# A list scheduler that counts TensorE's tile changes, operand changes and weight loads

## The chip, the cores and the metric

The kernel runs on one core of a Trainium2 chip. The metric is device time in microseconds (us) of one execution; the median of three runs is given, and one further execution was profiled. TensorE (PE) multiplies matrices; its weight loads are listed apart (PEld). VectorE (DVE), ScalarE (ACT) and GpSimd (POOL) do elementwise work; SyncE (SP) issues nearly all transfers.

## The reference, cut to what matters

One layer of a hybrid backbone over 640 tokens: 512 noisy grid tokens that see a cached context, and 128 prompt tokens. An adaLN-modulated input is projected by one wide matrix; four mixers run side by side (latent attention MLA, bidirectional mLSTM, windowed attention SWA, bidirectional RWKV-7); each passes an output matrix and a sigmoid gate; their sum passes `w_out`; a squared-ReLU MLP follows.

```python
h = rmsnorm(x, P['norm1'][l]) * (1.0 + scale1) + shift1
u = h @ P['w_in'][l]                       # 1024 x 8752, split into the mixers' inputs and 4 x 1024 gates
...
def step(Sm, inp):                         # RWKV-7, one token, one head (64 x 64 state)
    sk = jnp.einsum('bhvk,bhk->bhv', Sm, kh_t)
    Sn = Sm * w_t[:, :, None, :] - sk[..., None] * (a_t * kh_t)[:, :, None, :] + v_t[..., None] * k_t[:, :, None, :]
    return Sn, jnp.einsum('bhvk,bhk->bhv', Sn, r_t)
...
merged = (gates[:, :, 0] * (y_a @ P['mla_w_o'][l]) + gates[:, :, 1] * (y_b @ P['mlstm_w_o'][l])
          + gates[:, :, 2] * (y_c @ P['swa_w_o'][l]) + gates[:, :, 3] * (y_d @ P['rwkv_w_o'][l]))
x = x + gate1 * (merged @ P['w_out'][l])
f = jnp.square(jax.nn.relu(h2 @ P['mlp_w1'][l])) @ P['mlp_w2'][l]
```

All is float32, with tight tolerances, so the large products are made in three passes of the fast float32r type (high times high, high times low, low times high), and the small ones in plain float32.

## The kernel before, in words

**Dense products.** Weights come in pieces of up to 528 columns: a transfer into one of 3 buffers `wr`, ScalarE makes the high part `wh`, GpSimd (the first 139 pieces) or VectorE the low part `wl` (6 buffers each). `dense_b` (L614) makes channel-major results, in rows named `pb`: 128 weight columns stationary, two halves of 320 tokens moving, 48 matmuls for 128 channels. `dense_t` (L634) makes token-major ones, rows `pt`: 128 tokens stationary, up to 264 weight columns moving. `pa` and `pwo` are the MLP's second product and the output projection, with 512 columns. All of them are float32r and use the whole 128 x 128 array.

**Small products** are plain float32 and mostly use part of the array. Each is two records in the profile. In the RWKV chain (`step`, L1101; rows `pst`) one chunk of 64 tokens of a head pair and a direction takes a product of `S` and `KR` (128 x 128), then `VU` with `Am` (64 x 64), a copy by ScalarE (`W1`, L1115), `W1` with `Am` (64 x 64), a copy by VectorE (`VU`, L1118), `VU` with `Am` and with `KBT` (128 rows by 64 columns), and an update of `S` by VectorE (L1124), from which the next chunk starts. Four head pairs run one after the other; in each, two directions run interleaved over 8 chunks that depend on each other, beside 2 of the prompt. `psf` transposes the state at a pair's end. Preparation (`pat`, `pkb`) and a triangular inverse (VectorE, `ltmp` and `xl`, then `ptp` and `px` in 32 x 32 tiles) go ahead of each pair. Later stages: SWA (`psc`, `pspt`, `pso`) beside mLSTM (`pms`, `pmo`), then MLA's projections (`pq`, `pkv`) and attention (`pas`, `pat` again, here with `avM` and `aPT`), then the merge (`pb` on `yh`, `yl`). The dense projections of the gates and of later mixers (`fill_all`, `late`) have two accumulators of their own and may run at any time in between, in the order of their weights' buffers.

**What sets the order.** The program is first recorded, and `order` (L168) then puts it in order by a list schedule: it plays all engines forward with durations from `cost` (L127) and latencies between engines (L36, L37), and lets each engine take, among the instructions that are ready, the one with the longest path to the end (`bl`, with additions for work that empties PSUM and for stores). On TensorE the played time knows that a matmul must wait for those in flight only where their parts of the array overlap (`busy`), and that the next one may start 0.02 us later (`free`, L462). It also plays the clock: `seen` adds up the columns of work in each window of 3.41 us, and a window after one with fewer than 3060 runs at half speed (`warm`, L408). Where the present window is about to miss that, it takes the ready matmul with the most columns per time (L428) instead. The order found is then fixed on every engine; semaphores alone decide the times.

## Time and profile before

| | |
|---|---|
| three runs, us | 1810.11, 1816.44, 1823.94 (median 1816.44) |
| profiled execution | 1829.33 us; span from its first to its last instruction 1827.4 us |
| mean granted TensorE clock | 0.960 |
| busy, share of the span | PE 95%, PEld 85%, DVE 53%, ACT 39%, POOL 26% |
| instructions of them | 11923, 11923, 2250, 1711, 488 |
| matmuls with the whole array, 320 columns (`pb` on `HH`, `HL`) | 3 x 1328, 321 to 325 ns each, start to end |

A matmul's length in the profile reaches over the start of the next one, so what a matmul costs is read from the distance between two starts. A form such as `128*64 128x64` is rows times columns of the array that it uses, then partitions by elements that it reads. "Idle" is time in which an engine ran nothing; the granted clock is the share of full speed that TensorE had.

### The profile page before, as it was taken

The numbers are of one execution on the slowest core, as the hardware profiler recorded it, in microseconds if no ns is written. First come the engines' busy times: TensorE is split into PE (matmuls) and PEld (weight loads), VectorE is DVE, ScalarE is ACT, GpSimd is POOL, SyncE is SP. The second block draws the span as 40 slices with busy tenths as digits, with TensorE's granted clock in tenths as the row PEclk, the third lists the DMA queues.
The fourth block names the chain that finished last, engine by engine and source line by source line (L and its number), as shares of the span: only waits on it lengthen the run. The fifth ranks groups of instructions, "written<-read, shape, count | busy, mean of one in ns | idle before, by whom it ended". The sixth has DMA issues, their size and how long they took to land.

```text
span 1827.4 us, 32001 instructions
## 1 busy us (share of the span) xinstructions
PE 1742.4 (95%) x11923; PEld 1551.1 (85%) x11923; DVE 968.7 (53%) x2250; ACT 716.9 (39%) x1711; POOL 471.9 (26%) x488
## 2 busy tenths in 40 slices
PE   6999899999999987999989999899999999999998
PEld 3998788888888876878887999799889899898997
DVE  4236937586363348665548654367744334343342
ACT  5543242333223224675635643354434223132231
POOL 3455543354233223331222211005100010202012
PEclk9999999898679998999999999999999999999999
DMA  8554352344224354533363211576512222222222
GB/s 291 153 180 122 103 132 74 90 118 108 64 59 122 114 170 149 168 89 65 86 159 105 74 41 56 167 253 221 173 45 81 68 77 70 81 76 75 76 74 94
DMA packets 243211, 206.66 MB, mean 113 GB/s; under 512 B 46086, under 2 KB 194360, under 8 KB 243056
## 3 DMA queue, kind: packets, MB, share of 16 engines
q1 hardware_dynamic: 242416, 204.07, 38.2%
q8 instruction: 94, 1.54, 0.4%
q0 software_dynamic: 640, 0.56, 0.1%
q14 instruction: 61, 0.50, 0.1%
HBM read 163.08 MB, written 41.49 MB: 112 GB/s over the span
## 4 chain that ended last, share of the span: by engine, by line
PE 57%; DVE 5%; DMA 5%; ACT 1%; issue 1%; SPq 0%; POOL 0%; POOLq 0%; DVEq 0%; ACTq 0%
PE pb L542 29%; PE pa L542 12%; PE pwo L542 2%; DMA out_new_mlstm_n<-co 2%; PE pst L542 2%; PE pas L542 2%; PE pat L542 2%; PE pat L565 1%; PE pso L542 1%; PE pmo L542 1%; PE psc L542 1%; PE pada L542 1%; DMA wr<-in_w_in 1%; PE pms L542 1%; PE pspt L565 0%
## 5 line engine op out<-in xcount | busy, mean ns | idle before, releaser
L542 PE MATMUL pb<-HH,wh 128*128 128x320 f32 x1328 | 364.1, 325 | 21.8 <-ACT spb L833 10.8
L542 PE MATMUL pb<-HL,wh 128*128 128x320 f32 x1328 | 359.5, 323 | 0.8 <-DVE HL L753 0.8
L542 PE MATMUL pb<-HH,wl 128*128 128x320 f32 x1328 | 356.0, 321 | 0.0
L589 ACT CAST wh<-wr 128x512 fp32r<-128x512 f32 (+2 forms) x298 | 183.5, 618 | 379.9 <-PE pa L542 144.2
L592 POOL TENSOR_TENSOR wl<-wr,wh 128x512 fp32r<-128x512 f32 (+2 forms) x139 | 187.4, 1352 | 415.0 <-ACT wh L589 307.8
L542 PEld LDWEIGHTS pb<-HH,wh 128*128 128x128 f32 x1328 | 237.5, 192 | 33.6 <-ACT spb L833 12.9
L542 PEld LDWEIGHTS pb<-HL,wh 128*128 128x128 f32 x1328 | 236.8, 192 | 7.3 <-issue 4.0
L542 PEld LDWEIGHTS pb<-HH,wl 128*128 128x128 f32 x1328 | 236.4, 192 | 6.3 <-issue 3.5
L592 DVE TENSOR_TENSOR wl<-wr,wh 128x512 fp32r<-128x512 f32 x159 | 117.4, 744 | 200.1 <-ACT wh L589 116.5
L1846 POOL TENSOR_TENSOR x<-x,yt 128x512 f32<-128x512 f32 x40 | 53.6, 1341 | 480.7 <-DVE yt L1845 473.7
L542 PE MATMUL pt<-wh,HH 128*128 128x256 f32 (+2 forms) x360 | 101.7, 318 | 7.8 <-DVE mift L860 5.4
L542 PE MATMUL pa<-wh,fh 128*128 128x512 f32 x320 | 108.1, 393 | 0.0
L542 PE MATMUL pa<-wh,fl 128*128 128x512 f32 x320 | 106.7, 393 | 0.0
L542 PE MATMUL pa<-wl,fh 128*128 128x512 f32 x320 | 104.9, 393 | 0.0
L542 PE MATMUL pt<-wh,HL 128*128 128x256 f32 (+2 forms) x360 | 97.9, 312 | 0.0
L542 PE MATMUL pt<-wl,HH 128*128 128x256 f32 (+2 forms) x360 | 96.8, 310 | 0.0
L1109 POOL TENSOR_SCALAR S<-S,DL 128x128 f32<-128x128 f32 x80 | 56.8, 714 | 126.9 <-DVE S L1124 100.3
L542 PEld LDWEIGHTS pt<-wh,HH 128*128 128x128 f32 x360 | 68.1, 206 | 13.6 <-DVE mift L860 3.0
L835 DVE COPY spb<-pb 128x320 f32<-128x320 f32 x46 | 22.4, 487 | 105.9 <-PE pb L542 105.7
L542 PE MATMUL pst<-VU,Am 128*64 128x64 f32 (+1 forms) x640 | 74.2, 242 | 0.9 <-DVE VU L1118 0.5
L542 PE MATMUL pb<-yh,wh 128*128 128x320 f32 x256 | 64.8, 318 | 10.0 <-ACT yh L1752 6.5
L542 PEld LDWEIGHTS pa<-wh,fh 128*128 128x128 f32 x320 | 60.1, 188 | 13.4
(535 smaller groups left out, 3587.0 us busy)
## 6 DMA issues: line engine op xcount, KB each, us to landing
wr<-in_mlp_w SPq DMA_DIRECT2D x128, 256.0 KB
wr<-in_w_in SPq DMA_DIRECT2D x122, 256.0 KB
wa<-in_ada_w SPq DMA_DIRECT2D x64, 256.0 KB
gtd<-spb SPq DMA_DIRECT2D x32, 320.0 KB
sg<-gtd SPq DMA_DIRECT2D x32, 320.0 KB
ara<-in_ada_w SPq DMA_DIRECT2D x16, 512.0 KB
sgd<-sg SPq DMA_DIRECT2D x16, 320.0 KB
la<-sgd SPq DMA_DIRECT2D x16, 320.0 KB
```

What stands on the lines that cost most here:

```text
L542: PE.matmul(out, lhsT, rhs, start=start, stop=stop)
L565: PE.transpose(out, in_, ident[: in_.shape[0], : in_.shape[0]])
L589: A.copy(hi[:, :n], raw[:, :n])
L592: e.tensor_tensor(lo[:, :n], raw[:, :n], hi[:, :n].bitcast(F32), op=ALU.subtract)
L835: V.tensor_copy(t[:, hs(h)], p)
L1109: G.tensor_scalar(sn, so_, DL[:, c : c + 1], None, op0=ALU.mult)
L1846: G.tensor_tensor(x2[tt][:, cs], x2[tt][:, cs], t, op=ALU.add)
```

## The change

It is all in `cost` and `order`. The price of a float32r matmul goes from n/2400 us (at least 0.107) + 0.003 to n/2300 + 0.008 (at least 0.111), that of a plain one from n/600 + 0.002 to the larger of n and (n + m)/2, over 600, + 0.005, m being the columns of the array. Each matmul gets a form: its tile, rows and columns rounded up to 32, 64 or 128, and whether it is plain float32. A matmul of another tile than the one before waits in the played time for all in flight and 0.14 us more; a plain one after another kind in the same tile 0.08 us more. The next matmul may start after the weight load (columns/1200 us, twice that for plain float32), no longer after 0.02. In the choice by columns per time, that charge counts as time. Where the window's work is not in danger, a ready matmul of another tile must have a path to the end that is over 40 us longer (`STAY`) to be taken.

```diff
--- before.py
+++ after.py
@@ -35,6 +35,7 @@
 
 LAT = {"PE": 0.3, "DVE": 0.195, "Activation": 0.195, "Pool": 0.195}
 TO_PE = 0.127
+STAY = 40.0
 DMA_START, DMA_END, DMA_RATE, DMA_GAP = 1.5, 0.95, 360e3, 0.641
 
 
@@ -144,9 +145,9 @@
         if "is_transpose=True" in str(i):
             return 0.109
         if "float32r" in str(i.ins[0].dtype):
-            return max(n / 2400, 0.107) + 0.003
-        return max(n / 600, 0.05) + 0.002
-        
+            return max(n / 2300 + 0.008, 0.111)
+        return max(n, (n + m) / 2) / 600 + 0.005
+
     n = max([free(q) for q in ins + outs] or [1])
     if eng == "Activation":
         if op == "InstLoadActFuncSet":
@@ -406,6 +407,14 @@
         passes = 2 if "is_transpose=True" in str(raw[a]) else 1 if "float32r" in str(i.dtype) else 4
         cols[a] = passes * n * (spot[a][1] - spot[a][0]) / 128
     warm = lambda t: seen.get(int(t / TICK) - 1, 0) >= 3060
+    fit = lambda n: 32 if n <= 32 else 64 if n <= 64 else 128
+    form, load = {}, {}
+    for a, (r0, r1, c0, c1) in spot.items():
+        slow = "is_transpose=True" not in str(raw[a]) and "float32r" not in str(raw[a].ins[0].dtype)
+        form[a] = (fit(r1 - r0), fit(c1 - c0)), slow
+        load[a] = (c1 - c0) / 1200 * (2 if slow else 1)
+    now = ((128, 128), False)
+    turn = lambda a: 0.14 if form[a][0] != now[0] else 0.08 if form[a][1] and not now[1] else 0.0
     while left:
         best = None
         for e in ENG:
@@ -425,7 +434,9 @@
         if e == "PE" and (0.937 or 0) and len(avail[e]) > 1:
             gap = 3060 - seen.get(int(t / TICK), 0)
             if (not warm(t) and 0) or gap > ((int(t / TICK) + 1) * TICK - t) * 2400 * 0.937 > 0:
-                j = max(range(len(avail[e])), key=lambda i: (cols[avail[e][i][1]] / dur[avail[e][i][1]], -avail[e][i][0]))
+                j = max(range(len(avail[e])), key=lambda i: (cols[avail[e][i][1]] / (dur[avail[e][i][1]] + turn(avail[e][i][1])), -avail[e][i][0]))
+            else:
+                j = min(range(len(avail[e])), key=lambda i: avail[e][i][0] + (STAY if form[avail[e][i][1]][0] != now[0] else 0.0))
         if j:
             _, a = avail[e].pop(j)
             heapq.heapify(avail[e])
@@ -449,7 +460,9 @@
         else:
             if e == "PE":
                 r0, r1, c0, c1 = spot[a]
-                t = max([t] + [x[4] for x in busy if x[0] < r1 and r0 < x[1] and x[2] < c1 and c0 < x[3]])
+                other = form[a][0] != now[0]
+                t = max([t] + [x[4] for x in busy if other or x[0] < r1 and r0 < x[1] and x[2] < c1 and c0 < x[3]]) + turn(a)
+                now = form[a]
                 start[a] = t
                 w = warm(t)
                 fin = t + dur[a] * (1 if w else 2)
@@ -459,7 +472,7 @@
                     seen[k] = seen.get(k, 0) + cols[a] * (y - x) / (fin - t)
                     k, x = k + 1, y
                 busy = [x for x in busy if x[4] > t + 0.02] + [(r0, r1, c0, c1, fin)]
-                free[e] = t + 0.02
+                free[e] = t + max(0.02, min(fin - t, load[a] * (1 if w else 2)))
             else:
                 fin = free[e] = t + dur[a]
         out[e].append(a)
@@ -477,6 +490,7 @@
             need2[b] -= 1
             if need2[b] == 0:
                 release(b)
+    order.span = max(free.values())
     info = mybir.DependencyInfo(mybir.DependencyClass.NoSync, mybir.DependencyReason.DATA)
     for e in ENG:
         for a, b in zip(out[e], out[e][1:]):
```

TensorE's order, in the chain of head pair 0. `pst_969` and `pst_974` are the same chunk step (the fifth) of the two directions; `pb` and `pt` are dense projections. A row with "x2" is two products. Before:

```order
L542 MATMUL pb_272_1963<-HL_65,wh_277_1995 128x320
L542 MATMUL pst_969_5901<-W1_970_5905,Am_756_4989 64x64 x2
L542 MATMUL pb_272_1963<-HH_64,wl_276_1994 128x320
L542 MATMUL pst_974_5923<-S_962_5875,KR_770_5053 128x128
L542 MATMUL pb_272_1963<-HH_64,wh_277_1995 128x320
L542 MATMUL pst_974_5923<-VU_973_5920,Am_772_5062 64x64 x2
L542 MATMUL pb_280_2028<-HH_64,wh_283_2031 128x320
L542 MATMUL pb_272_1963<-HL_65,wh_277_1995 128x320
L542 MATMUL pb_280_2028<-HL_65,wh_283_2031 128x320
L542 MATMUL pst_969_5901<-VU_968_5898,Am_756_4989 64x64 x2
L542 MATMUL pst_969_5901<-VU_968_5898,KBT_757_4990 64x64 x2
```

Now, the same small products:

```order
L556 MATMUL pt_244_1717<-wl_230_1665,HH_64 128x264
L556 MATMUL pst_974_5923<-S_962_5875,KR_770_5053 128x128
L556 MATMUL pst_969_5901<-W1_970_5905,Am_756_4989 64x64 x2
L556 MATMUL pst_974_5923<-VU_973_5920,Am_772_5062 64x64 x2
L556 MATMUL pt_244_1717<-wh_234_1672,HH_64 128x264
L556 MATMUL pt_242_1689<-wh_234_1672,HH_64 128x264
L556 MATMUL pt_244_1717<-wh_234_1672,HL_65 128x264
L556 MATMUL pt_242_1689<-wh_234_1672,HL_65 128x264
L556 MATMUL pst_969_5901<-VU_968_5898,Am_756_4989 64x64 x2
L556 MATMUL pst_969_5901<-VU_968_5898,KBT_757_4990 64x64 x2
```

Before, single dense products stand between the small ones, and the tile changes five times in these rows. Now the three small products of the two directions stand side by side, the dense ones come four at a time, and the tile changes three times; the dense work beside this step is another piece of the projections (`pt`) than before (`pb`).

TensorE's order in MLA's attention, for one pair of heads: `aPT` holds the transposed probabilities, `avM` the values, `pat_2572` is where their products add up. Before:

```order
L542 MATMUL pat_2572_13271<-avM_10832,aPT_2569_13258 128x64
L542 MATMUL pb_2232_11643<-HH_64,wh_2235_11646 128x320
L542 MATMUL pat_2572_13271<-avM_10832,aPT_2569_13258 128x64
L542 MATMUL pb_2233_11644<-HL_65,wh_2235_11646 128x320
L542 MATMUL pat_2572_13271<-avM_10832,aPT_2569_13258 128x64
L542 MATMUL pb_2232_11643<-HL_65,wh_2235_11646 128x320
L542 MATMUL pat_2572_13271<-avM_10832,aPT_2569_13258 128x64
L542 MATMUL pb_2233_11644<-HH_64,wl_2234_11645 128x320
L542 MATMUL pat_2572_13271<-avM_10832,aPT_2569_13258 128x64 x2
```

Now:

```order
L556 MATMUL pas_2600_13414<-akT_10831,qTm_2398_12374 128x128
L556 MATMUL pb_2188_11314<-HL_65,wh_2193_11346 128x320
L556 MATMUL pat_2572_13271<-avM_10832,aPT_2569_13258 128x64 x3
L579 MATMUL pat_2581_13320<-k0_68,aP_2578_13311 128x128 x4
L556 MATMUL pat_2572_13271<-avM_10832,aPT_2569_13258 128x64 x6
L579 MATMUL pat_2582_13326<-k0_68,aP_2576_13300 128x128
L579 MATMUL pat_2582_13326<-k0_68,aP_2578_13311 128x128
L556 MATMUL pat_2572_13271<-avM_10832,aPT_2569_13258 128x64
L556 MATMUL pb_2187_11313<-HL_65,wh_2193_11346 128x320
```

Before, each product with `avM` (plain float32) has a dense `pb` (float32r) behind it. Now they come three and six in a row, behind transposes, and the dense work stands together.

Over the whole order, the dense products that stand ahead of some points change, too: ahead of the end of chain 2 (the last `psf` of head pair 2) there were 745 `pb` and 1080 `pt`, and now there are 663 and 480.

## The prediction

> **What bounds the kernel now.** I read the page first, then the stretches, then the chain of waits and the waits by engine, then single matmuls in order of time.

> The page's head, and its rows of 40 slices for TensorE and its clock:

> ```profile
> span 1827.4 us, 32001 instructions
> PE 1742.4 (95%) x11923; PEld 1551.1 (85%) x11923; DVE 968.7 (53%) x2250; ACT 716.9 (39%) x1711; POOL 471.9 (26%) x488
> PEclk9999999898679998999999999999999999999999
> ```

> TensorE is busy for 95% of the span, so its instruction stream sets the time. The clock's row has one deep hole, in slices 11 and 12 (457 to 548 us). The busy times by stretch of the span:

> ```profile
> core 0: us, PE busy (x) PEld busy (x) DVE busy (x) ACT busy (x) POOL busy (x), PEclk, DMA share, GB/s
> 115.00:557.00 442.00, 424.96 (x3514) 371.13 (x3513) 287.31 (x618) 142.51 (x316) 190.84 (x183) 0.90 0.37 99
> 360.00:428.00 68.00, 67.70 (x650) 57.25 (x649) 55.47 (x138) 22.77 (x63) 37.17 (x36) 1.00 0.35 100
> 428.00:557.00 129.00, 125.59 (x936) 108.86 (x935) 71.03 (x168) 37.93 (x87) 40.56 (x47) 0.71 0.32 81
> 557.00:650.00 93.00, 91.47 (x822) 74.18 (x821) 28.41 (x82) 27.37 (x76) 28.82 (x36) 1.00 0.44 119
> 920.00:1028.00 108.00, 99.67 (x615) 88.70 (x614) 64.68 (x227) 56.21 (x170) 25.56 (x25) 0.97 0.45 113
> 1028.00:1172.00 144.00, 144.00 (x1113) 142.69 (x1112) 78.91 (x200) 60.37 (x154) 16.06 (x13) 1.00 0.21 61
> 1172.00:1210.00 38.00, 29.96 (x184) 26.14 (x182) 18.71 (x30) 18.38 (x30) 1.29 (x1) 0.91 0.84 276
> 1210.00:1827.00 617.00, 604.96 (x3426) 549.09 (x3426) 283.09 (x485) 204.05 (x398) 87.06 (x72) 1.00 0.32 99
> ```

> 115 to 557 us holds the RWKV preparation and the chains of head pairs 0 to 2; 557 to 650 the chain of pair 3; 1028 to 1172 the latent attention; from 1210 the merge, the output projection and the MLP. In that last third every matmul is full size and TensorE is busy 605 of 617 us: the change finds no work there. In the RWKV stretch TensorE looks busy too (425 of 442), while VectorE is busy 287, a share of 0.65. Who waits for whom there, by the waits of the whole span:

> ```profile
> ACT W L1115 <- PE pst L542: 77.0, 61, 4.5
> DVE S L1124 <- PE pst L542: 37.4, 33, 2.6
> PE pst L542 <- DVE VU L1118: 0.5, 2, 0.3
> ```

> ScalarE and VectorE wait for the chain's matmuls (77 and 37 us); the matmuls hardly wait for VectorE (0.5 us). TensorE paces the recurrence: dense projections that stand between its small matmuls hold it up, and half of the clock is gone in part of it.

> **The price of a change of tile and of operand.** Matmuls in order of time, in the chain of pair 3; a row's start less the next row's start is what it cost on TensorE. A product of plain f32 operands leaves two records, so "x2" of `pst` is one product.

> ```profile
> 637.81 0.30 PE L542 MATMUL pb<-HH,wl 128*128 128x320 f32 x1
> 638.05 0.45 PE L542 MATMUL pst<-VU,Am 128*64 128x64 f32 x4
> 638.42 0.33 PE L542 MATMUL pst<-W,Am 64*64 64x64 f32 x2
> 638.68 0.33 PE L542 MATMUL pst<-VU,KBT 128*64 128x64 f32 x2
> 638.93 0.33 PE L542 MATMUL pst<-W,Am 64*64 64x64 f32 x2
> 639.19 0.33 PE L542 MATMUL pst<-VU,KBT 128*64 128x64 f32 x2
> 639.45 1.90 PE L542 MATMUL pada<-wa,csl 128*32 128x512 f32 x10
> 641.28 0.45 PE L542 MATMUL pst<-VU,Am 128*64 128x64 f32 x4
> 641.57 0.28 PE L542 MATMUL pst<-VU,KBT 128*64 128x64 f32 x2
> ```

> Where two shapes alternate (638.42 to 639.45) a product takes 1.03/4 = 0.26 us. Where the shape stays (641.28 to 641.57) two take 0.29, or 0.145 each. A change of tile costs 0.26 - 0.145, say 0.11 us. The step into the small tile (637.81 to 638.05, 0.24) against the dense price below gives 0.09. For the dense price, a long run in the chain of waits, and dense matmuls of the token-major form in order of time:

> ```profile
> 1385.60 31.89 PE pb L542 x216
> 431.01 0.40 PE L542 MATMUL pt<-wh,HH 128*128 128x256 f32 x2
> 431.25 0.40 PE L542 MATMUL pt<-wh,HL 128*128 128x256 f32 x2
> 431.49 0.41 PE L542 MATMUL pt<-wl,HH 128*128 128x256 f32 x2
> ```

> A `pb` is 31.89/216 = 0.148 us, a `pt` (431.49 - 431.01)/4 = 0.12. And in the attention, where f32 products stand between dense ones:

> ```profile
> 1108.44 0.33 PE L542 MATMUL pat<-avM,aPT 128*128 128x64 f32 x2
> 1108.58 0.39 PE L542 MATMUL pb<-HL,wh 128*128 128x320 f32 x1
> 1108.81 0.33 PE L542 MATMUL pat<-avM,aPT 128*128 128x64 f32 x2
> ```

> The same `pb` takes 0.23 when an f32 product follows: 0.08 us more, while the next weights load. [...]

> **The change, part by part.** The new costs, the charge for a turn and the preference all act through one thing, the order on the engines; no instruction is added or removed. Counted over the whole of TensorE's order: changes of tile 667 before, 497 now (170 fewer); steps into an f32 product from another kind in the same tile 382 before, 257 now (125 fewer). At 0.11 and 0.08 that is 18.7 + 10 = 29 us of TensorE's own time. It isn't the sum, because the order also moves work between stages:

> 1. *Up to the end of chain 2.* 112 of the 170 tile changes and 10 of the operand steps fall away here (13 us), and 82 `pb` and 600 `pt` fewer stand ahead of that point (82 x 0.148 + 600 x 0.12 = 84 us), all to be done later. Of the 442 us now, 0.90 of the clock was granted, so at full clock TensorE needs at most 398; less 84 and 13 is 301. VectorE's 287 us stay, bar a few evacuations of the moved projections. So TensorE stops pacing the stretch and VectorE starts. How densely VectorE can run no row shows directly; bounds are 0.65 (the whole stretch) and 0.95, where its 302 us meet TensorE's 301. I take 0.82, the best long stretch seen (360 to 428: 55.47/68), since that one has the same chain, inverse and preparation in it. 287/0.82 = 350: the end of chain 2 comes at 465 instead of 557, 92 us earlier. New waits of TensorE are in these 350.
> 2. *The moved work,* +84 us. It lies in the chain of pair 3 and behind it (600 of the 682 are `pt`, dense, at full clock). The weight loads on SyncE's queue, the splits on ScalarE, GpSimd and VectorE and the evacuations go with their matmuls; 84 us of dense work carry them as the dense stretches now do. In chain 3 VectorE has 28 of 93 us, so TensorE goes on pacing there.
> 3. *Behind chain 2:* 58 tile changes and 115 operand steps fewer, 6.4 + 9.2 = 16 us; 98 of the steps are in the attention.
> 4. *Holes that get filled.* The chain of waits has two stage borders where TensorE ran dry:

> ```profile
> 928.15 7.59 DMA out_new_mlstm_n<-co
> 937.24 3.43 DMA wr<-in_mla_w_uq
> 1181.34 5.76 DMA yb<-yT
> 1199.10 8.01 DMA sg<-gtd
> ```

> Idle there: 108 - 99.67 = 8 us and 38 - 29.96 = 8, with 0.03 x 108 + 0.09 x 38 = 7 of clock on top, 23 in all. The new order has 580 `pb` instead of 173 between the last `pmo` and the first `pq`, and 292 instead of 56 between the last `pat` and the first product on `yh`: 86 and 43 us of dense cover. Bounds 0 and 23; I take 15, since the wait for `sg` comes after the cover.
> 5. *The attention* loses 152 `pb` of its filler (22 us). Its 144 us have TensorE fully busy, so nothing shows its own chain as the pace; I take it as 22 shorter, the work being in the 292 above. If its softmax chain needs the 144, 22 + 8 = 30 us come back.

> Sum: -92 + 84 - 16 - 15 = -39 us. The profiled execution took 1829.3 (span 1827.4 and 1.9 around it), so 1790 by it; its time lies 13 above the median of 1816.4, and the forecast on the median is **1777**.

> **The rivals.**
> *VectorE stays at 0.65.* The chain's hops between engines pace the stretch; TensorE now waits, in order, in front of each `pst`, with no dense work left there to fill the wait. Then chain 2 still ends at 557, and the 84 us come on top: -39 + 92 = +53, 1869. It turns at 287/(504 - 115) = 0.74: below it the kernel is slower. For it: the order shown above leaves four dense matmuls (4 x 0.12 = 0.5 us) ahead of a product that waits for a copy. Against it: VectorE reached 0.82 beside a fully loaded TensorE. Chance 0.09.
> *The clock stays low.* Row 428 to 557 has 0.71 where small matmuls thin the stream out. If the whole stretch gets that, TensorE's 301 become 424, chain 2 ends at 539, +35, 1851. [...] Against it as a loss: a TensorE that waits for VectorE anyway loses little by a slow clock. 0.06.
> *VectorE does not bind* (0.95, limit 301): chain 2 ends at 417, 48 more, -87, 1729. 0.20 for this side, -65 and better.
> *Nothing to measure:* VectorE at 0.70 to 0.77, the waits eat the grouping. 0.17.
> That the grouping isn't reached at all is out: the order shows it.

> **How the numbers follow.** My case, -18 to -65, has 0.48. Within 1% (18 us, what a measurement of this kernel can tell) is 0.17; faster is 0.48 + 0.20 = 0.68; slower 0.15. The range goes from the value of the third rival, 1730, to 1828, and leaves out about 0.06 below and 0.13 above.

> **What would show it.** Right: chain 2's last `psf` near 465 and VectorE at about 0.8 up to there; TensorE's waits for `VU`, `W` or `S` grown from nearly nothing to tens of us; PEclk's hole smaller or under those waits; the idle time around `yb` and `mla_w_uq` gone; the stretch from 1210 to the end as long as now, 617 us. Wrong: chain 2 ending after 505, or an attention that still takes 144 us.

## The result, and the profile after

The kernel became slower. The median of four runs is 1877.99 us (1864.35 to 1884.26), against 1816.51 (1810.11 to 1823.94) for four runs of the kernel before: a ratio of 1.0327, 95% interval 1.0258 to 1.0396. The forecast was 1777. The profiled execution took 1864.35 us, 35 more than the profiled one of before. These two stand closer together than the medians, 61 apart, because the one is the fastest of its kernel and the other the slowest; the stages below are read from them.

The head of the page after, and its clock in 40 slices:

```profile
span 1862.6 us, 32016 instructions
PE 1749.8 (94%) x11923; PEld 1565.2 (84%) x11923; DVE 967.9 (52%) x2250; ACT 720.1 (39%) x1711; POOL 471.5 (25%) x488
PEclk9998977676799999999999999999999999999999
```

The hole in the clock has moved and widened: before it was two slices deep (457 to 548 us), now it is six slices long (233 to 512). The mean granted clock fell from 0.960 to 0.939. The clock records of both traces hold only full and half clock (1.0 and 0.5), so that is 2 x 0.040 x 1827 = 146 us at half clock before and 2 x 0.061 x 1863 = 227 after. TensorE's idle time, span less busy, went from 85 to 113 us.

TensorE's transposes of the state at the end of chain 2, in order of time, first after, then before:

```profile
506.39 0.48 PE L579 MATMUL psf<-k,S 128*128 128x128 f32 x1 [0.95 <-ACT ys L1141]
508.65 0.42 PE L579 MATMUL psf<-k,S 128*128 128x128 f32 x1
```

```profile
552.39 0.27 PE L565 MATMUL psf<-k,S 128*128 128x128 f32 x1
553.53 0.27 PE L565 MATMUL psf<-k,S 128*128 128x128 f32 x1
```

Chain 2 ends at 509 us instead of 554 (the prediction's 557 was a round edge behind it), and the same transpose takes 0.42 to 0.48 us instead of 0.27. The busy times by stretch, the columns as in the prediction, after:

```profile
core 0: us, PE busy (x) PEld busy (x) DVE busy (x) ACT busy (x) POOL busy (x), PEclk, DMA share, GB/s
115.00:509.00 394.00, 355.16 (x2802) 303.84 (x2803) 279.29 (x595) 121.17 (x272) 159.61 (x158) 0.77 0.33 86
608.00:690.00 82.00, 73.50 (x537) 69.10 (x537) 62.95 (x141) 35.91 (x86) 38.06 (x41) 0.94 0.51 145
690.00:861.00 171.00, 155.81 (x1061) 137.63 (x1061) 104.90 (x375) 104.66 (x356) 36.19 (x64) 0.96 0.34 84
861.00:979.00 118.00, 105.65 (x706) 93.10 (x705) 26.46 (x108) 37.14 (x106) 32.50 (x27) 0.97 0.68 175
1045.00:1166.00 121.00, 120.98 (x940) 117.46 (x939) 75.62 (x195) 55.07 (x144) 11.25 (x9) 1.00 0.15 40
1166.00:1210.00 44.00, 43.97 (x300) 43.21 (x299) 10.99 (x16) 15.75 (x27) 11.19 (x9) 1.00 0.77 259
```

The same stages before (chains 0 to 2; from the end of chain 3 to mLSTM; mLSTM; its border to MLA; attention; its border to the merge):

```profile
115.00:554.00 439.00, 421.96 (x3485) 368.55 (x3483) 286.12 (x613) 139.57 (x313) 190.84 (x183) 0.90 0.36 98
648.00:744.00 96.00, 80.23 (x488) 67.24 (x488) 63.51 (x140) 36.28 (x87) 32.78 (x38) 0.86 0.55 168
744.00:909.00 165.00, 159.49 (x1109) 140.98 (x1108) 104.20 (x372) 105.48 (x349) 41.14 (x66) 0.98 0.38 92
909.00:949.00 40.00, 31.52 (x190) 29.54 (x190) 12.66 (x51) 13.19 (x49) 11.62 (x9) 0.91 0.63 138
1029.00:1170.00 141.00, 141.00 (x1094) 139.93 (x1093) 77.31 (x198) 58.50 (x150) 15.42 (x12) 1.00 0.21 60
1170.00:1189.00 19.00, 11.89 (x80) 9.03 (x78) 5.14 (x9) 8.50 (x15) 1.29 (x1) 0.93 0.82 279
```

The first row of each tells most. Before, the stretch of the chains took 439 us: 88 of them (2 x 0.10 x 439) at half clock, 17 idle, so its work at full clock is about 422 - 88/2 = 378. After, 394 us: 181 at half clock, 39 idle, work 355 - 181/2 = 264. (The traces' own clock records give 92 and 177 us for the rounded 88 and 181.) So 114 us of work left the stretch, and it became only 45 us shorter: half clock took back (181 - 88)/2 = 47, idle time 22. The work that left was mostly moved and had to be done later: from the end of chain 2 to the end of the span it is 1353.6 us instead of 1273.4, 80 more. 80 - 45 = 35.

Waits of the whole span after:

```profile
ACT W L1129 <- PE pst L556: 59.2, 47, 3.6
DVE S L1138 <- PE pst L556: 26.3, 28, 5.2
PE pst L556 <- DVE VU L1132: 7.5, 12, 1.0
```

ScalarE and VectorE still wait for TensorE's chain products (77 and 37 us before), TensorE now also for VectorE (0.5 before).

### The profile page after: what moved, and what is told of

Its sections match the earlier page's. It is cut to its first block, busy times and chain, and to the rows that moved or that the text cites. A ratio compares the mean times of both kernels' runs of the same rounds, so it can differ in the third digit from the quotient of the medians.

```text
span 1862.6 us, 32016 instructions
## 1 busy us (share of the span) xinstructions
PE 1749.8 (94%) x11923; PEld 1565.2 (84%) x11923; DVE 967.9 (52%) x2250; ACT 720.1 (39%) x1711; POOL 471.5 (25%) x488
## 4 chain that ended last, share of the span: by engine, by line
PE 76%; DVE 11%; DMA 6%; ACT 2%; issue 2%; SPq 1%; POOL 1%; POOLq 0%; ACTq 0%; DVEq 0%
PE pb L556 32%; PE pa L556 12%; PE pt L556 6%; PE pst L556 6%; PE pat L556 3%; PE pwo L556 3%; PE pas L556 2%; DMA out_new_mlstm_n<-co 2%; PE pada L556 2%; DVE xl L1068 2%; DVE ltmp L1063 1%; PE pmo L556 1%; PE pat L579 1%; PE pso L556 1%; DMA wa<-in_ada_w 1%
## 5 line engine op out<-in xcount | busy, mean ns | idle before, releaser
L556 PEld LDWEIGHTS pb<-HH,wl 128*128 128x128 f32 x1328 | 240.6, 194 | 7.3 <-issue 4.6
L556 PE MATMUL pa<-wl,fh 128*128 128x512 f32 x320 | 115.6, 394 | 0.0
L556 PE MATMUL pa<-wh,fh 128*128 128x512 f32 x320 | 115.6, 394 | 0.0
L556 PE MATMUL pa<-wh,fl 128*128 128x512 f32 x320 | 114.6, 394 | 0.0
L556 PE MATMUL pst<-VU,Am 64*64 64x64 f32 (+1 forms) x640 | 81.7, 264 | 7.5 <-DVE VU L1132 7.5
L556 PEld LDWEIGHTS pst<-VU,Am 64*64 64x64 f32 (+1 forms) x640 | 59.5, 163 | 26.5 <-DVE VU L1132 9.7
L556 PEld LDWEIGHTS pa<-wl,fh 128*128 128x128 f32 x320 | 60.1, 188 | 13.0 <-DVE wl L606 0.2
```

The costliest lines, as they stand in the source:

```text
L556: PE.matmul(out, lhsT, rhs, start=start, stop=stop)
```

## The experiments

Three theories. CLOCK: dense work left the chains' stretch, and the small products alone don't hold the clock. PREFERENCE: holding a product back for the sake of the tile (`STAY`) delays the chains. HOPS: the chains are paced by VectorE and by the way from engine to engine, whatever the clock does.

For all runs one table. "Half clock" is 2 x (1 - mean granted clock) x span, "idle" the span less TensorE's busy time, both of the profiled execution. "Order" gives tile changes / operand steps. "Priced" is what the matmuls of the order would take without waits, if each cost the median distance of starts that its kind and its successor's kind have in the trace before. Span = priced + half of the half clock + idle, up to a rest of -9 to 29 us.

| run | ratio to before, 95% interval | span | order | priced | half clock | idle |
|---|---|---|---|---|---|---|
| before | 1 | 1827 | 667/382 | 1656 | 146 | 85 |
| after | 1.0327 (1.0258 to 1.0396) | 1863 | 497/257 | 1617 | 227 | 113 |
| e1_preference | 0.9854 (0.9795 to 0.9912) | 1787 | 574/387 | 1639 | 86 | 92 |
| e2_prices | 1.0479 (1.0430 to 1.0528) | 1912 | 650/231 | 1634 | 344 | 104 |
| e3_after_dense | 1.0268 (1.0215 to 1.0322) | 1867 | as after | 1652 | 157 | 115 |
| e4_before_dense | 1.0064 (1.0015 to 1.0114) | 1843 | as before | 1691 | 114 | 86 |
| e5_after_thin | 1.0654 (1.0622 to 1.0687) | 1956 | as after | - | 426 | 95 |
| e6_after_lift | 1.0452 (1.0426 to 1.0479) | 1901 | 493/303 | 1623 | 213 | 159 |
| e7_preference_kind | 1.0259 (1.0218 to 1.0299) | 1862 | 553/175 | 1629 | 175 | 154 |
| e8_turn | 1.0175 (1.0113 to 1.0237) | 1851 | 670/353 | 1654 | 211 | 84 |
| e9_after_fill6000 | 1.0243 (1.0186 to 1.0299) | 1866 | 540/286 | 1628 | 198 | 125 |
| e10_after_fill6400 | 1.0080 (1.0054 to 1.0106) | 1828 | 533/269 | 1625 | 113 | 117 |
| e11_costs | 1.0055 (1.0023 to 1.0087) | 1823 | 655/382 | 1655 | 135 | 79 |
| e12_load | 1.0059 (1.0017 to 1.0101) | 1818 | 662/231 | 1648 | 120 | 83 |

The medians of the prices take in starts at half clock, so kinds that mostly ran there are priced too high: of the 240 `pt` products with 208 columns 126 did, and their median is 0.21 us where those at full clock took 0.11. From starts at full clock alone the rows come out some 25 to 40 us lower (before 1622 to 1627, after 1586 to 1588, by how finely kinds are told apart), and the rest as much larger; the differences between rows stay within 10 us of those shown.

The ranges of the theories were set for a before of 1816 us; in the experiments before took 1816 to 1826, so a range is to be read to within 10 us.

By this table the new order is 39 us cheaper; half clock costs it 41 more (81/2) and idle time 28 more. The profiled execution may show the clock's part too small: the other three executions of after were granted 0.925 to 0.931, 259 to 282 us at half clock.

**One part at a time.** The preference alone, against after:

```diff
-            return max(n / 2300 + 0.008, 0.111)
-        return max(n, (n + m) / 2) / 600 + 0.005
+            return max(n / 2400, 0.107) + 0.003
+        return max(n / 600, 0.05) + 0.002
-    turn = lambda a: 0.14 if form[a][0] != now[0] else 0.08 if form[a][1] and not now[1] else 0.0
+    turn = lambda a: 0.0
-                other = form[a][0] != now[0]
+                other = False
-                free[e] = t + max(0.02, min(fin - t, load[a] * (1 if w else 2)))
+                free[e] = t + 0.02
```

> The preference for the same tile alone, with the old prices, no charge for a turn and the old next-start of 0.02 us. Its order has 574 tile changes (667 before, 497 after the change) and 720 pb and 1031 pt ahead of the end of chain 2 (before 745 and 1080, after 663 and 480). Theory CLOCK (the change loses because the dense projections leave the RWKV stretch, whose small matmuls then run at half clock): the dense work stays, so the clock stays as before, and 93 tile changes x 0.11 us are won, some 10 to 20 us: 1795 to 1808. Theory PREFERENCE (holding chain steps back for the tile's sake is what costs): slower than before, 1830 to 1880. Theory HOPS (VectorE and the hops between engines pace the stretch): as CLOCK, 1795 to 1816.

Its median was 1796.14 us, 1.5% faster than before, within the ranges of CLOCK and of HOPS. The chains' stretch and the border from mLSTM to MLA in its trace:

```profile
114.00:511.00 397.00, 380.06 (x3388) 333.80 (x3387) 286.54 (x598) 135.23 (x305) 184.00 (x178) 0.94 0.39 105
874.00:910.00 36.00, 27.94 (x172) 26.32 (x171) 10.14 (x40) 11.29 (x42) 7.87 (x6) 0.91 0.55 118
```

Chain 2 ends at 511, two microseconds behind after's, with 586 more matmul records ahead of it, at a clock of 0.94 and with 17 us idle. PREFERENCE falls. The counterpart is the change without the preference:

```diff
-STAY = 40.0
+STAY = 0.0
```

> The whole change but with STAY at 0: new prices, turns and weight loads, no preference. 650 tile changes, 648 pb and 480 pt ahead of the end of chain 2. CLOCK: dense work is as thin as after the change, so the same half clock and 153 tile changes x 0.11 = 17 us less won: 1880 to 1900. PREFERENCE: the loss goes, 1800 to 1820. HOPS: 1875 to 1895.

1911.44 us, more than any of the three theories gave: the prices and charges do the harm, and the preference takes some of it back. They were then run one by one, each with the other edits undone: the charge for a turn with the wait for all in flight (of the change, only the lines with `turn` and `other`), the two prices (only the lines in `cost`), the weight load (only the line with `free[e]`).

> Of the change only the charge of 0.14 and 0.08 us for a tile change and an operand step, and the wait for all in flight at a tile change; prices, weight load and preference as before the change. The order has 670 tile changes and 353 operand steps, 720 pb and 605 pt ahead of the end of chain 2 (1080 pt before). CLOCK: with 475 transposes fewer beside the chains the half clock up to the end of chain 2 is 120 us or more and the whole is 1850 to 1890 us. HOPS (VectorE and the hops pace the chains): hardly a step of a chain changes its length: 1815 to 1840 us.

> Of the change only the two new prices of a matmul; no charge for a turn, no weight load, no preference. The order has 655 tile changes and 382 operand steps (as good as before), and 720 pb and 904 pt ahead of the end of chain 2 (745 and 1080 before), so that only the dense work moves. CLOCK: half clock up to the end of chain 2 of 110 to 160 us and a whole of 1825 to 1850 us, with no grouping to pay for it. HOPS (it is grouping or charges that harm the chain steps): 1810 to 1825 us, no difference from before.

> Of the change only the last piece not run alone yet: the next matmul may start after the weight load in the played time (no longer after 0.02 us); prices, turn charge, wait for all in flight and preference as before the change. The order has 662 tile changes (667 before), 231 operand steps (382) and 720 pb and 898 pt ahead of the end of chain 2 (745 and 1080). By the distances between starts of the trace before, priced at the full clock, its matmuls need 1648 us in place of 1656. CLOCK: about as with the two prices alone, which move as much dense work: half clock up to the end of chain 2 of 100 to 140 us and a whole of 1820 to 1850 us, with TensorE's waits about as before. HOPS in its narrower form (the charged time makes the scheduler place small products ahead of the moment at which the chip has their operands, so TensorE waits in order): TensorE's waits at full clock grow by 25 us or more over the span, half clock or not, and the whole is 1845 us or more.

The turn charge came to 1856.80 us, the prices to 1827.09, the weight load to 1830.22. Half clock up to the end of chain 2 was 147, 85 and 89 us: for the first as expected, for the other two below what was expected (at least 110 and 100); the whole lies in CLOCK's range for all three, for the prices only 2 us above HOPS's. Each moves dense `pt` products behind the chains (605, 904 and 898 of 1080 stay), and the one that moves most loses most, with hardly a tile change less and no more idle time (84, 79 and 83 us). That speaks for CLOCK, and against the narrower HOPS of the last expectation. The three together, e2, lose more than their sum (4.8% against 2.9%); two of the three terms of that sum, 0.6% each, are only just clear of none.

**The clock by itself.** In after, the order fixed, four transposes were put ahead of the `S` x `KR` products of each chain step; nobody reads them. The same was done to before.

```diff
+            for _ in range(4):
+                pools.warm.add(PE.transpose(ps[:, 384:512], ident, ident).ins.name)
...
+    out["PE"] = [x for a in out["PE"] for x in (*ahead.get(a, ()), a)]
```

> The changed kernel, every engine's order as it is, with four transposes of the identity (128 x 128, into unused columns of the step's own PSUM tile, read by nobody) put ahead of each of the 80 chain steps' S x KR products: 320 x 0.109 = 35 us of work for TensorE that computes nothing. CLOCK: the extra work keeps the clock up; half-clock time up to the end of chain 2 falls from 177 us to below 60, chain 2 ends 10 to 45 us earlier than at 509, total 1835 to 1868 against 1878. HOPS: the work fills waits at best, chain 2 ends at 509 or up to 35 us later, 1878 to 1913.

> The kernel before, its order as it is, with the same 320 transposes. CLOCK: the 92 us of half clock up to the end of chain 2 fall below 30, which gives back up to 46 of the work's own 35 us: 1805 to 1830. HOPS: the work comes on top, 1835 to 1851.

After with them took 1870.43 us, 2 us above CLOCK's range and 8 below HOPS's, and before with them 1841.81, in HOPS's range and 12 above CLOCK's. Half clock up to the end of chain 2 fell less far than CLOCK said: to 106 us (below 60 expected) and to 48 (below 30), and chain 2 of after ended at 504, 5 us earlier. About 35 us of priced work were added to each, for 5 and 16 us of span. Free filling of waits would do that too, so the control keeps their number and place and lowers the columns from 128 to 32:

```diff
-                pools.warm.add(PE.transpose(ps[:, 384:512], ident, ident).ins.name)
+                pools.warm.add(PE.matmul(ps[:, 384:416], HH[:, 0, 0:128], HH[:, 0, 0:32], start=True, stop=True).ins.name)
```

> The order after, fixed; ahead of the S x KR products of each chain step TensorE also runs 4 products of one 128x128 float32r weight with only 32 columns (unused PSUM columns, read by nobody). They fill the same places as the 320 transposes of the run with added transposes behind the order after, and hold TensorE about as long each (a weight load), but carry a quarter of the columns or less. CLOCK (the small matmuls run at half clock because little runs through the array, and the added transposes paid for themselves by lifting the clock): no clock is won, about 27 us are added; chain 2 ends 25 to 35 us later than in the run with transposes, near 530 to 545 us, half clock up to there 170 us or more, the whole 1895 to 1915 us. HOPS (the added transposes were free because TensorE waits there anyway): these are free too; chain 2 ends near 505 to 510 us and the whole is 1870 to 1880 us.

1937.31 us, above the ranges of both. The stretches up to the end of chain 2, first with transposes, then with thin products:

```profile
112.00:504.00 392.00, 356.50 (x3077) 309.20 (x3075) 285.68 (x600) 123.41 (x276) 162.87 (x162) 0.87 0.34 89
```

```profile
112.00:588.00 476.00, 456.48 (x3072) 398.80 (x3072) 281.65 (x600) 124.23 (x276) 158.98 (x160) 0.63 0.28 73
```

The added products alone in the two traces (duration in ns, least, median and most; then first and last start):

```profile
L1134 PE MATMUL pst<-k x320: 270/273/473, 123.9 to 605.8; 128*128 128x128 f32 x160
```

```profile
L1134 PE MATMUL pst<-HH x320: 178/374/397, 123.5 to 696.6; 128*128 128x32 f32 x160
```

One order, as many added instructions in the same places; from start to start the transposes took 45 us in all and the thin ones 55. At one clock they cost the same, 0.109 and 0.112 us at full and 0.213 each at half, but 224 of the thin ones ran at half clock and 47 of the transposes. The chains end 84 us apart, at a clock of 0.87 and of 0.63. TensorE is busy for 456 of the 476 us. The profiled execution took 21 us more than the median; if all of that lay ahead of chain 2's end, 63 of the 84 would be left. The other executions show the same: the four others with thin products were granted 0.905 to 0.917 over the whole span, the four with transposes 0.954 to 0.959. HOPS as the sole pace falls: the chains do slow down with the clock. The runs of one kernel fit that: 15 runs of before on one chip had 101 to 153 us of half clock, and a straight line through them gives 0.40 us of span per us of it (correlation 0.97).

**Bringing the dense work back.** All prices kept, with 50 us more path length for the products of the RWKV projections:

```diff
+        elif op[k] == "InstMatmult" and raw[k].outs[0].bass_ap.tensor.name[:3] in ("pb_", "pt_"):
+            bl[k] += 50
```

> The whole change (prices, charge for a tile change, wait for all in flight, weight load counted, preference for the tile), but the products and transposes of the RWKV projections (pb, pt) get 50 us more of path length, so that the scheduler starts them early again: 720 pb and 907 pt instead of 480 pt stand ahead of the end of chain 2, with as few tile changes (493) as after. CLOCK (the loss comes from the dense work leaving the chains' stretch): half clock up to the end of chain 2 falls from 177 us to under 110 us, and the whole comes to 1785 to 1815 us. HOPS (the chain steps themselves got longer through the new order, whatever stands between them): 1855 to 1885 us.

The half clock from the chains' start to the end of chain 2 fell to 90 us (177 after), as CLOCK said, and chain 2 ended at 513; the whole, 1900.68 us, was worse than after and above the ranges of both. The other try was a stronger preference alone, which holds to the operand's kind too:

```diff
-STAY = 40.0
+STAY = 100.0
...
+                j = min(range(len(avail[e])), key=lambda i: avail[e][i][0] + (STAY if form[avail[e][i][1]] != now else 0.0))
```

> Of the change only the preference, now for the same tile and the same kind of operand (plain float32 or not), and with 100 us in place of 40 us; prices, turn charge and weight load as before. The order has 553 tile changes and 175 operand steps in place of 667 and 382, and the dense work ahead of chain 2 as before (746 pb, 1080 pt). CLOCK: as nothing dense leaves the chains' stretch, the half clock there stays under 60 us and the tile changes and operand steps saved show: 1775 to 1795 us. HOPS (a preference of 100 us holds chain steps up): 1830 to 1870 us.

Here, too, the stretch came out as CLOCK expected (half clock 55 us, the end of chain 2 at 528) and the whole didn't: 1864.95 us, in HOPS's range, whose reason, chain steps held up, doesn't fit a chain 2 that ends 26 us earlier than before. The border from mLSTM to MLA and that from attention to merge in e7, then the second of these in e6:

```profile
942.00:975.00 33.00, 3.53 (x12) 1.51 (x11) 9.70 (x46) 8.76 (x36) 0.00 (x0) 0.50 0.29 82
1206.00:1224.00 18.00, 1.46 (x6) 0.98 (x5) 4.21 (x7) 6.91 (x11) 0.00 (x0) 0.50 0.70 236
```

```profile
1229.00:1247.00 18.00, 1.86 (x8) 1.11 (x7) 4.44 (x8) 6.99 (x11) 0.00 (x0) 0.50 0.70 236
```

In e1 TensorE was busy for 27.94 of 36 us at the first border (above), in after for 43.97 of 44 at the second; here it runs 12, 6 and 8 matmul records, at half clock. The orders say why. Between the last `pmo` and the first `pq` stood 173 dense products before, 165 in e1 and none in e7; between the last `pat` and the first product on `yh` 56 before, 292 after, and none in e7 and e6. The 857 that e7 runs from the end of chain 3 to the last `pmo` (before 573) are missing at the borders; e6 spends 452 in the attention (before 360). The filler is one stock for all stages: what an order spends early is missing later. Idle time over the span is 159 us in e6 and 154 in e7, half clock behind chain 2 118 and 119 (before 51).

The last try leaves the stock alone and changes what the scheduler aims at when a window is about to run thin:

```diff
-            gap = 3060 - seen.get(int(t / TICK), 0)
+            gap = 6400 - seen.get(int(t / TICK), 0)
```

> The whole change, and one number beside it: the scheduler takes dense work early where the present window of its played time is about to miss 6000 columns, in place of 3060 (the window from which it counts the clock as full stays at 3060). 720 pb and 1015 pt stand ahead of the end of chain 2 (after: 663 and 480; before: 745 and 1080), and the order keeps 540 tile changes and 286 operand steps (after: 497 and 257; before: 667 and 382). Nothing else is lifted, so that the later stages keep their cover. CLOCK (the loss is the half clock beside the chains once dense work has left them): half clock up to the end of chain 2 under 90 us, the whole 1770 to 1805 us. HOPS (the chain steps themselves got longer through the new order): 1850 to 1885 us.

> As the run with 6000, with 6400: 876 pb and 1080 pt ahead of the end of chain 2, more dense work than before the change, with 533 tile changes and 269 operand steps. CLOCK: half clock up to the end of chain 2 under 60 us; the end of chain 2 comes at 530 to 555 us, as more work stands ahead of it, and the whole is 1760 to 1800 us. HOPS: 1850 to 1885 us.

With 6000 it was 1864.41 us, with 6400 1829.57; both miss the range of CLOCK, and the first lies in that of HOPS. Half clock from the chains' start to the end of chain 2 was 116 and 65 us, above the 90 and 60 expected, and with 6400 chain 2 ended at 569, 14 us behind CLOCK's range. The stretch of the chains with 6400:

```profile
113.00:569.00 456.00, 415.11 (x3663) 367.45 (x3662) 288.87 (x615) 147.85 (x322) 190.79 (x188) 0.93 0.38 102
```

Half clock in the whole run is down to 113 us, half of after's and within the 101 to 153 of before's runs, and with it 35 us of span are won back from after. But TensorE is idle for 41 of these 456 us where before had 17 of 439, with more matmul records in the stretch than before. By the table its order is 31 us cheaper than before's (22 to 25 by starts at full clock) and half clock costs it 16 less; 32 us more idle time and a rest that is 16 larger eat that. By their ranges for the whole, neither theory holds: CLOCK met four of the twelve runs (e1, e8, e11, e12), HOPS four (e1, e4, e7, e9). CLOCK is one part of the answer, the larger one; the other part are waits that the new order doesn't cover. Whether they come from small products standing side by side or from charged time that makes the scheduler reckon with operands too early was not told apart. The preference alone groups (93 tile changes fewer) with 7 us more idle time, and each charge alone brings none; the three charges together without the preference (e2) bring 19. That is most of after's 28, but which wait it is stays open.

## Why the prediction was wrong

**The saving itself is there, by the prices.** From the tile changes and operand steps 29 us of TensorE's own time were forecast; the order's priced work fell by 39, 1656 to 1617 (34 to 39 by starts at full clock). No run changed the price of a tile change alone.

The 0.08 us of an operand step were measured rightly: in the trace before, 100 `pb` with a product of `avM` behind them have a median of 0.231 us to its start, and 3977 with another `pb` behind them 0.147. What makes them is less sure than "while the next weights load" has it. The weight loads of that product, in the same trace:

```profile
1108.66 0.34 PEld L542 LDWEIGHTS pat<-avM,aPT 128*128 128x128 f32 x2
```

The first of the two starts 0.08 us after the `pb` (1108.58), while that runs, and 0.15 us ahead of its own product (1108.81). It is recorded as 0.19 us long and so ends 0.04 us behind that product's start. That the load's length makes the 0.08 us is an estimate from these rows; no run shows it.

**Term 1 failed, at the step "so TensorE stops pacing the stretch and VectorE starts".** "The end of chain 2 comes at 465 instead of 557" rested on VectorE running at a share of 0.82. It came to 279/394 = 0.71 and the end to 509. The step before it held: TensorE's work there, forecast as 301, was even less, 264. But the sum took this work at full clock and put the loss to the clock at nothing. TensorE was busy for 355 of 394 us: thinned out, it got a clock of 0.77 and used up at half clock 47 us of what had been taken from it; idle time took 22. That is 45 us won instead of 92. The bound of 0.82 was read from a stretch (360 to 428) with a granted clock of 1.00, and the thinning itself took that condition away.

**The clock's rival was thrown out by a wrong argument.** "A TensorE that waits for VectorE anyway loses little by a slow clock" gave it 0.06. The runs with transposes and thin products refute it: 84 us between two clocks (63 at least), one order. Nor did half clock come with long gaps in the matmul stream: in the prediction's row from 428 to 557 TensorE was busy for 125.59 of 129 us at a clock of 0.71, and no idle stretch there was longer than 1.6 us. The rival's sum, +35 on the profiled execution, is what was measured, partly by chance: it put chain 2's end at 539 (509 measured) and the rest of the span 53 longer (80 measured), and on the medians the loss is 61.

**Terms 2 and 3** gave 84 - 16 = 68 us more behind chain 2; priced by starts at full clock the orders give 60 to 64, so the sizes were about right. (By the table's prices it is 88, as the 240 `pt` of 208 columns, priced too high there, have all moved behind chain 2.) What left the stretch was forecast as 97 (84 + 13); it is 98 by these prices and 114 by the clock's rows.

**Term 4, the holes,** was to give 15 and gave nothing in sum: TensorE's idle time behind chain 2 was 53 us before and is 59 now. The border from attention to the merge is filled as forecast (idle 7.1 us, now 0.03). That from mLSTM to MLA is not: idle 8.5 before, 12.3 now, in spite of its dense cover. A row of TensorE's waits there, after:

```profile
PE pada L556 <- DMA wa<-in_ada_w: 7.7, 1, 7.7
```

The wait for an adaLN weight took the place of the old one. In mLSTM idle time grew from 5.5 to 15.2 us; between the end of chain 3 and mLSTM it fell from 15.8 to 8.5. Terms 2 to 4 came to 53 us in the sum, and 80 were measured. Some 62 of the 80 are priced work and 5 idle time; half clock there gave back 2, and some 15 no run explains.

**Term 5 was right:** the attention takes 121 us instead of 141, 20 shorter where 22 was forecast. Its own test, "an attention that still takes 144 us", didn't show; the other, "chain 2 ending after 505", did.

**The share of VectorE.** The measured 0.71 lies in the rival "Nothing to measure" (0.70 to 0.77; 0.17), beside "VectorE stays at 0.65" (0.09). The turning point of 0.74 held: 0.71 lies below it, and the kernel is slower. But with an end at 509 the prediction's sum gives -39 + 44 = +5; of the other 30, 27 lie behind chain 2 and 3 in the round edge of 557. The mechanism of the 0.65 rival, hops between the engines with a TensorE that waits, could account for the 22 us of idle time here, not for the rest.

## What to carry to other kernels

When dense filler is moved away from a latency-bound chain, ask first what the clock does with the thin stream that is left, and give that rival its full price: an engine that looks freed can be slowed until it paces again (here the clock of the chains' stretch went from 0.90 to 0.77). Filler is one stock for all the stretches that need cover, so a scheduling rule is judged by how much dense work is left in each of them, before its saved switches are counted. And test the parts of such a change apart: here one of four, the preference for the tile with the old prices, gained 1.5% (0.9854, 0.9795 to 0.9912), while the whole lost 3.3%; it is the fastest version that was run.

## What the runs showed of the hardware that was not expected

**A busy TensorE can be a slow one.** In the thin run the added product of 32 columns took 374 ns at the median and the transpose in its place 273, though it has four times the columns: most of the thin ones ran at half clock (224 of 320), few of the transposes (47). More columns made the same stream faster: up to the end of chain 2 it took 392 us with the transposes and 476 with the thin products.

**The spread between runs goes with the clock.** The 0.40 us of span per us of half clock, from 15 runs of one kernel, is close to the half that a TensorE busy throughout would lose; on three other chips the same line gives 0.35 to 0.42 (8 to 12 runs each). No run shows what makes the half clock differ from run to run.
